# Hybrid streaming encoder on one core: the mixer's key-decay products move from GpSimd to VectorE, ScalarE's exponentials and gates are held in order, norm weights are folded, caches and rotary key go ahead of the query latent

## The chip, the core and the metric

The kernel is one program on one core of a Trainium2 chip. The metric is the device time of one launch in microseconds (us). A core has a matrix engine (TensorE, PE in the tables, with PEld for its weight loads), VectorE (DVE), ScalarE (ACT), GpSimd (POOL) and SyncE (SP), whose queue issues the transfers. Each engine runs its own list of instructions strictly in order; an instruction that has to wait for another engine holds up everything behind it in its list.

## The reference

Two groups of tokens (512 of a new stream, 64 of a running one) pass two layers of an encoder that share all weights. In each layer stand a feed-forward block, a mixer and a second feed-forward block. The mixer projects the normalised input once and splits it among three head groups:

```python
z = h @ w_in[l]
q_a, kv_a, kpe_raw, hq, hf, hi, hg, cu, cv = jnp.split(z, offsets, axis=-1)
# HGRN2, in chunks of 64: b = cumulative sum of log forget gates
diff  = b[:, :, None] - b[:, None, :]
decay = exp(diff) where causal, else 0
A     = einsum('bthe,btshe,bshe->bhts', qc, decay, kc)
S_new = exp(b_last) * S + einsum('bshe,bshd->bhed', kc * exp(b_last - b), vc)
o_b   = rmsnorm(o, out_g) * silu(hg)
# chunk MLP: u = gelu(cu); v = rmsnorm(gelu(cv)) * v_g; o_c = u * (w_s v + b_s)
# latent attention: q from rmsnorm(q_a), keys from rmsnorm(kv_a) and the rotated kpe_raw
mix = concat([o_a, o_b, o_c], axis=-1) @ w_out[l]
```

## The kernel before, in words

All 576 tokens stand as columns; a float32 product is made of three fast products of split operands (`split`: ScalarE writes the high part `hi`, VectorE the rest `lo`; `three`, `nat3`: hi·hi, hi·lo, lo·hi). `together`, `unit` and `natural` multiply by pieces of a weight; `cols`, `nat_chunks` and `chunk` load such a piece (`wr`) and split it into `wh` and `wl`.

The order of the program is made in two steps. The Python code is one main thread that issues matrix products, and a list of generators (`spawn`, `tick`): a generator goes on when the clock `self.t`, an estimate of TensorE's time, has passed the value that it yielded. Then a scheduler of the framework takes all instructions and sets each engine's list by priorities and its own estimates. An instruction passed through `keep_in_program_order` may not move ahead of what the Python code gave the same engine before it.

`mixer` runs in four stages. **First**, `natural` multiplies five tiles of tokens by 512, 512 and 320 columns of `w_in` (tile `n` of TensorE): `vg` (values and gate), `uv` (the chunk MLP's inputs) and the latents of the keys. Beside it runs the generator `hgrn`: the decay matrix A is built by seven levels of halving (`LEVELS`), two halves of the heads each, so 14 items. `make(n)` subtracts the cumulative sum around each block's middle (`e`, two VectorE instructions L701 and L702), takes the exponential on ScalarE (L703), multiplies the keys by it on GpSimd (`w`, L705) and the queries by it on VectorE (`zb`, two instructions L711). `use(n)` multiplies both on TensorE (`lv`, `ls`) and copies the entries of this level into A (L726, L733). `self.pace` is the time between items. **Second**, three `unit` calls make the query latent (`u`); beside them run the states (`su`, `st`), the outputs `out` (`o`, `on`), and `cmlp` (`cm`, `oc`): both call `group_norm`, whose inverse root is made on GpSimd (`rsqrt`, tile `gr`); `to_mix` transposes the results (`tp`). `gates` makes GELU (L882) and SiLU (L886). `latent` makes the key latents (`cn`, `rk`). **Third**, `caches` and `rotary_key` are spawned behind the query latent (`ck`, `kp`, `kd`), then values (`v`) and rotated queries (`rope`: `sw` on ScalarE and GpSimd, `qr`). **Fourth** come `query`, keys, attention and the output projection.

Of the kernel before, what the change touches and what calls it, by code (L numbers as in the profile page):

```python
# [8 lines left out]
F32 = mybir.dt.float32  # L9
# [6 lines left out]
P = 128  # L16
# [33 lines left out]
class Net:  # L50
    def __init__(self, tc, i, o):
        self.tc = tc
        self.nc = tc.nc
        self.i = i
        self.o = o
        self.count = 0
        self.bg = []
        self.t = 0.0
        self.pace, self.apace, self.l1, self.l2, self.l3 = 3.0, 2.16, 1.26, 3.94, 2.15
# [565 lines left out]
    def group_norm(self, src):  # L625
        nc = self.nc
        sq = self.slot("gsq")
        nc.scalar.activation(sq[:, :256], src, AF.Square)
        ss = self.small("gs", 4)
        nc.vector.tensor_reduce(ss, sq[:, :256].rearrange("p (g d) -> p g d", g=4), AX.X, ALU.add)  # L630
        nc.vector.tensor_scalar(ss, ss, 1.0 / 64, EPS, op0=ALU.mult, op1=ALU.add)
        r = self.small("gr", 4)
        self.rsqrt(r, ss, 4)
        return r.unsqueeze(2).to_broadcast([P, 4, 64])

    def to_mix(self, src, k0, i):
        ps = self.sm("tp")
        for e in range(2):
            self.flip(ps[:, e * P:(e + 1) * P], src[:, e * P:(e + 1) * P])
        c, w = tcol(i), twid(i)  # L640
        for e in range(2):
            self.split(self.mixh[k0 + e][:, c:c + w], self.mixl[k0 + e][:, c:c + w], ps[:, e * P:e * P + w])
# [7 lines left out]
    def hgrn(self, l, zq, zf, vg):  # L650
# [36 lines left out]
        for m in range(2):  # L687
            qk.append(self.slot("qk"))
            nc.gpsimd.tensor_tensor(qk[m], q[m], kk[m], op=ALU.mult)
# [3 lines left out]
        def make(n):  # L693
            li, h, m = items[n]
            c0 = 64 if h == 64 else 0
            nb = (T - c0) // (2 * h)
            e = self.slot("e")
            bv = b[m][:, c0:].rearrange("p (b x) -> p b x", x=2 * h)
            ev = e[:, c0:].rearrange("p (b x) -> p b x", x=2 * h)
            rb = bv[:, :, h - 1:h].to_broadcast([P, nb, h])  # L700
            nc.vector.tensor_tensor(ev[:, :, :h], rb, bv[:, :, :h], op=ALU.subtract)  # L701
            nc.vector.tensor_tensor(ev[:, :, h:], bv[:, :, h:], rb, op=ALU.subtract)  # L702
            nc.scalar.activation(e[:, c0:], e[:, c0:], AF.Exp)  # L703
            w = self.slot("w")
            nc.gpsimd.tensor_tensor(w[:, c0:], kk[m][:, c0:], e[:, c0:], op=ALU.mult)  # L705
            z = zbuf[n % 3]
            qv = q[m][:, c0:].rearrange("p (b x) -> p b x", x=2 * h)
            for g in range(2):
                rs = slice(g * 64, (g + 1) * 64)
                zo = z[rs, g, c0 // 2:].rearrange("p (b x) -> p b x", x=h)  # L710
                nc.vector.tensor_tensor(zo, qv[rs, :, h:], ev[rs, :, h:], op=ALU.mult)  # L711
            ready[n] = (w, z)
# [60 lines left out]
        for m in range(2):  # L773
# [5 lines left out]
            nc.scalar.activation(e, e, AF.Exp)  # L779
            eb[m] = self.slot("eb")  # L780
            nc.scalar.activation(eb[m], b[m], AF.Exp)
            nc.gpsimd.tensor_tensor(e, e, kk[m], op=ALU.mult)
# [18 lines left out]
        for i in (1, 2, 3, 4, 0):  # L801
            for m in range(2):
# [16 lines left out]
                yield 0.1  # L819
# [4 lines left out]
        def out(i):  # L824
# [10 lines left out]
            if rows < P:  # L835
# [3 lines left out]
            nc.vector.tensor_tensor(on[:, :256].rearrange("p (g d) -> p g d", g=4),  # L839
                                    ps[:, :256].rearrange("p (g d) -> p g d", g=4), r, op=ALU.mult)  # L840
            nc.vector.tensor_tensor(on[:, :256], on[:, :256], vg[i][:, 256:512], op=ALU.mult)
            yield 7.71
            self.to_mix(on, 4, i)
# [7 lines left out]
    def cmlp(self, l, i, t, c):  # L851
# [3 lines left out]
        vv = v.rearrange("p (g d) -> p g d", g=4)  # L855
        nc.vector.tensor_tensor(vv, vv, r, op=ALU.mult)
        nc.gpsimd.tensor_tensor(v, v, c["vg"], op=ALU.mult)
# [19 lines left out]
    def gates(self, l, c, vg, uv):  # L877
# [3 lines left out]
        for i in range(5):  # L881
            nc.scalar.activation(uv[i][:, :512], uv[i][:, :512], AF.Gelu_apprx_tanh)  # L882
            self.spawn(self.cmlp(l, i, uv[i], c), 0.8 + 2.59 * i)
        for i in range(5):
            g = vg[i][:, 256:512]
            nc.scalar.activation(g, g, AF.Silu)  # L886
            nc.gpsimd.tensor_tensor(g, g, c["og"], op=ALU.mult)
# [3 lines left out]
    def latent(self, l, i, ps, c, r, kr, cth, ctl):  # L891
# [15 lines left out]
        yield 4.0  # L907
# [138 lines left out]
    def mixer(self, l, gpost, gpre, nxt, packed):  # L1046
# [15 lines left out]
        c["og"] = self.gain_rows("hgrn_out_g", l)  # L1062
# [29 lines left out]
        for i in range(5):  # L1092
            ps = self.natural(nch, i, 320)
            lat.append(self.spawn(self.latent(l, i, ps, c, r, kr, cth, ctl)))
            self.step(self.bg[-1])

# [15 lines left out]
        cg = self.spawn(self.caches(l, c), 0.0)  # L1112
        lat.append(self.spawn(self.rotary_key(l, kr, a), 1.0))
# [171 lines left out]
    def bounds(self, more):  # L1285
        nc = self.nc
        ps = self.sm("tp")
        self.flip(ps[:, :18], more)
        nc.vector.tensor_copy(self.colg[:, 96:], ps[:, :18])
# [19 lines left out]
    def build(self):  # L1309
# [10 lines left out]
        pin = tc.keep_in_program_order  # L1320
# [26 lines left out]
        self.colg = const.tile([P, 114], F32, name="colg", tag="colg")  # L1347
# [30 lines left out]
        more = const.tile([18, P], F32, name="more", tag="more")  # L1378
        nc.sync.dma_start(more[0:6], i["mla_qa_g"].rearrange("l (k p) -> (l k) p", p=P))
        nc.sync.dma_start(more[6:10], i["hgrn_lb_logits"].rearrange("l (k p) -> (l k) p", p=P))  # L1380
        nc.sync.dma_start(more[10:18], i["cmlp_b_s"].rearrange("l g t -> (l g) t"))
        self.bs = self.colg[:, 106:114]
        self.spawn(self.pre_stats(0, 0.17, sums))
# [78 lines left out]
```

## Time and profile before

| | us |
|---|---|
| three runs, median (lowest to highest) | 2287.99 (2287.04 to 2290.99) |
| the profiled execution, its own time | 2284.6 |
| its span | 2282.8 |
| TensorE busy in the span | 2214.3 (97%) |
| VectorE busy | 1554.9 (68%) |
| ScalarE busy | 1093.4 (48%) |
| GpSimd busy | 225.6 (10%) |

Between the span and the execution's own time lie 1.8 us of start and end. The two mixers take about 307 us each, from 451 to 757 and from 1575 to about 1890; the other time is feed-forward blocks, where TensorE hardly ever waits. A matrix product's row shows its whole way through the engine, so consecutive rows overlap: what one costs is read from the distance of starts, or from a chain row ("x65" in so many us). "idle before" in square brackets is the time in which the engine had nothing to do, with what ended it. PEclk is the granted clock as a share of full speed.

### The profile page before, as it was taken

To read this page: it belongs to the slowest core of one execution; us is meant where nothing else is said; L and a number is where in the kernel's file an instruction comes from. 1 tells how busy PE (TensorE), PEld (TensorE's weight loads), DVE (VectorE), ACT (ScalarE), POOL (GpSimd) and SP (SyncE) were. 2 spreads that over 40 slices of the span, in tenths; PEclk is the share of its full clock that TensorE was granted. 3 is DMA by queue.
4 is the path that set the end of the run, shared out by engine and by line. 5 is a ranking of instruction groups with operands and counts; after the bars stand their busy time and mean duration, and the time that the engine had idled before them with its cause. 6 is when DMAs were issued, how large, how long until landed. Compare 5 with 4: busy or idle time off the path is not lost.

```text
span 2282.8 us, 39582 instructions
## 1 busy us (share of the span) xinstructions
PE 2214.3 (97%) x15988; PEld 2157.1 (94%) x15988; DVE 1554.9 (68%) x2627; ACT 1093.4 (48%) x1917; POOL 225.6 (10%) x230
## 2 busy tenths in 40 slices
PE   9999999998899999999999999999988999999998
PEld 8999999888799999999999999998887999999998
DVE  6787643787666888845597875447975678887443
ACT  7444442466554644443354444324645645444423
POOL 0000000343301100000020000004332020000000
PEclk9999999999999999999999999999999999999999
DMA  7333442312112333344133334423121232333421
GB/s 218 93 93 93 120 135 84 98 53 78 54 57 79 107 93 93 94 129 125 56 98 93 93 89 133 127 65 102 40 87 48 63 112 72 98 93 101 122 70 42
DMA packets 339531, 211.06 MB, mean 92 GB/s; under 512 B 17378, under 2 KB 319700, under 8 KB 339348
## 3 DMA queue, kind: packets, MB, share of 16 engines
q1 hardware_dynamic: 339348, 208.54, 30.6%
q8 instruction: 125, 2.05, 0.4%
q14 instruction: 58, 0.48, 0.1%
HBM read 190.11 MB, written 18.38 MB: 91 GB/s over the span
## 4 chain that ended last, share of the span: by engine, by line
PE 80%; DVE 10%; ACT 3%; issue 3%; POOL 3%; DMA 0%; SPq 0%; POOLq 0%; DVEq 0%; ACTq 0%
PE d L68 24%; PE X L68 20%; PE Q L68 10%; PE u L68 8%; PE R L68 5%; PE wo L68 4%; DVE zb L711 2%; PE n L68 2%; PE sc L68 1%; DVE x L256 1%; DVE hl L142 1%; DVE d L253 1%; DVE wl L127 1%; PE q L68 1%; PE oT L68 1%
## 5 line engine op out<-in xcount | busy, mean ns | idle before, releaser
L68 PE MATMUL d<-gh,wh 128*128 128x288 f32 x1408 | 413.5, 297 | 2.7 <-ACT gh L138 2.7
L68 PE MATMUL d<-gl,wh 128*128 128x288 f32 x1408 | 413.9, 295 | 0.0
L68 PE MATMUL d<-gh,wl 128*128 128x288 f32 x1408 | 412.7, 294 | 0.0
L127 DVE TENSOR_TENSOR wl<-wr,wh 128x1024 fp32r<-128x1024 f32 (+3 forms) x190 | 224.0, 1183 | 177.7 <-ACT wh L126 176.2
L126 ACT ACTIVATE wh<-wr 128x1024 fp32r<-128x1024 f32 (+3 forms) x190 | 191.5, 1011 | 297.2 <-PE d L68 166.9
L68 PEld LDWEIGHTS d<-gh,wh 128*128 128x128 f32 x1408 | 262.3, 187 | 3.6 <-ACT gh L138 3.6
L68 PEld LDWEIGHTS d<-gh,wl 128*128 128x128 f32 x1408 | 264.8, 188 | 0.0
L68 PEld LDWEIGHTS d<-gl,wh 128*128 128x128 f32 x1408 | 264.1, 188 | 0.0
L68 PE MATMUL X<-th,wh 128*128 128x288 f32 x864 | 255.7, 296 | 0.0
L68 PE MATMUL X<-tl,wh 128*128 128x288 f32 x864 | 254.9, 295 | 0.0
L68 PE MATMUL X<-th,wl 128*128 128x288 f32 x864 | 254.0, 294 | 0.0
L68 PE MATMUL u<-hh,wh 128*128 128x288 f32 x736 | 223.4, 305 | 3.1 <-ACT x L1368 1.5
L138 ACT ACTIVATE wh<-wr 128x1024 fp32r<-128x1024 f32 x144 | 152.1, 1056 | 154.2 <-PE R L68 68.5
L68 PE MATMUL u<-hl,wh 128*128 128x288 f32 x736 | 223.0, 303 | 1.2 <-DVE hl L142 1.2
L68 PE MATMUL u<-hh,wl 128*128 128x288 f32 x736 | 221.7, 302 | 0.0
L139 DVE TENSOR_TENSOR wl<-ws,wh 128x1024 fp32r<-128x1024 f32 x108 | 132.5, 1226 | 100.5 <-ACT wh L138 100.2
L139 DVE TENSOR_TENSOR wl<-wr,wh 128x1024 fp32r<-128x1024 f32 x144 | 175.6, 1222 | 15.8 <-ACT wh L138 14.4
L151 POOL TENSOR_TENSOR p<-m,mhalf 128x3 f32<-128x3 f32 (+1 forms) x14 | 14.4, 1030 | 1713.8 <-DVE m L234 1507.8
L395 DVE TENSOR_TENSOR d<-d,d 128x288 f32<-128x288 f32 x128 | 55.3, 455 | 182.0 <-PE d L68 181.9
L138 ACT ACTIVATE wh<-ws 128x1024 fp32r<-128x1024 f32 x108 | 114.6, 1061 | 132.6 <-DVE ws L502 96.1
L68 PEld LDWEIGHTS X<-th,wl 128*128 128x128 f32 x864 | 162.8, 188 | 0.0
L68 PEld LDWEIGHTS X<-tl,wh 128*128 128x128 f32 x864 | 162.2, 188 | 0.0
(364 smaller groups left out, 5781.8 us busy)
## 6 DMA issues: line engine op xcount, KB each, us to landing
wr<-ffn_w_gate SPq DMA_DIRECT2D x144, 256.0 KB, 3.0
wr<-ffn_w_up SPq DMA_DIRECT2D x144, 256.0 KB, 3.4
wr<-ffn_w_down SPq DMA_DIRECT2D x64, 512.0 KB, 4.2
wr<-w_in SPq DMA_DIRECT2D x30, 512.0 KB, 3.7
xd<-x SPq DMA_DIRECT2D x48, 288.0 KB, 2.4
x<-xd SPq DMA_DIRECT2D x48, 288.0 KB, 5.5
wr<-ffn_w_down SPq DMA_DIRECT2D x32, 384.0 KB, 3.5
wr<-ffn_w_gate SPq DMA_DIRECT2D x16, 512.0 KB, 3.9
```

Of the source, the lines that this page charges most:

```text
L68: self.nc.tensor.matmul(out, lhsT, rhs, start=start, stop=stop, skip_group_check=onto)
L126: nc.scalar.activation(hi[:, :a * b], raw[:, :a * b], AF.Copy)
L127: nc.vector.tensor_tensor(lo[:, :a * b], raw[:, :a * b], hi[:, :a * b].bitcast(F32), op=ALU.subtract)
L138: nc.scalar.activation(hi, src, AF.Copy)
L139: nc.vector.tensor_tensor(lo, src, hi.bitcast(F32), op=ALU.subtract)
L142: nc.vector.scalar_tensor_tensor(lo, src, scale, hi.bitcast(F32), op0=ALU.mult, op1=ALU.subtract)
L151: self.nc.gpsimd.tensor_tensor(out, m, self.mhalf[:, :n], op=ALU.pow)
L253: nc.vector.scalar_tensor_tensor(d[s][:, sl], d[s][:, sl], gpost[s], bc, op0=ALU.mult, op1=ALU.mult)
L256: nc.vector.tensor_tensor(self.x[k][:, sl], self.x[k][:, sl], d[k][:, sl], op=ALU.add)
L395: nc.vector.tensor_tensor(d[m][:, sl], d[m][:, sl], ps[hf][:, :n], op=ALU.add)
L711: nc.vector.tensor_tensor(zo, qv[rs, :, h:], ev[rs, :, h:], op=ALU.mult)
```

## The change

The products of the keys with the decay (L689, L705, L782) go from GpSimd to VectorE; the one of the levels is written over `e` and only into the half of each block that is used, so tile `w` is gone. Five kinds of ScalarE instruction, the exponentials of the levels and of the states, GELU and SiLU, are passed through `keep_in_program_order` (`self.pin`). The norm of each group is applied by four instructions of 64 columns that take the factor and the weight (or the gate) at once. `hgrn_out_g` is no longer multiplied into the gate by GpSimd, but applied as a column scale in `to_mix`'s split. `caches` and `rotary_key` are spawned ahead of the query latent. Four waiting times change: `pace` 3.0 to 2.2, and the yields of the states (0.1 to 0.6), of the latents (4.0 to 8.0) and the rotary key (1.0 to 6.0).

```diff
-        self.pace, self.apace, self.l1, self.l2, self.l3 = 3.0, 2.16, 1.26, 3.94, 2.15
+        self.pace, self.apace, self.l1, self.l2, self.l3 = 2.2, 2.16, 1.26, 3.94, 2.15
...
-    def to_mix(self, src, k0, i):
+    def to_mix(self, src, k0, i, scale=(None, None)):
...
-            self.split(self.mixh[k0 + e][:, c:c + w], self.mixl[k0 + e][:, c:c + w], ps[:, e * P:e * P + w])
+            self.split(self.mixh[k0 + e][:, c:c + w], self.mixl[k0 + e][:, c:c + w], ps[:, e * P:e * P + w], scale=scale[e])
...
-            nc.gpsimd.tensor_tensor(qk[m], q[m], kk[m], op=ALU.mult)
+            nc.vector.tensor_tensor(qk[m], q[m], kk[m], op=ALU.mult)
...
-            nc.scalar.activation(e[:, c0:], e[:, c0:], AF.Exp)
-            w = self.slot("w")
-            nc.gpsimd.tensor_tensor(w[:, c0:], kk[m][:, c0:], e[:, c0:], op=ALU.mult)
+            self.pin(nc.scalar.activation(e[:, c0:], e[:, c0:], AF.Exp))
...
-            ready[n] = (w, z)
+            kv = kk[m][:, c0:].rearrange("p (b x) -> p b x", x=2 * h)
+            nc.vector.tensor_tensor(ev[:, :, :h], ev[:, :, :h], kv[:, :, :h], op=ALU.mult)
+            ready[n] = (e, z)
...
-            nc.scalar.activation(e, e, AF.Exp)
+            self.pin(nc.scalar.activation(e, e, AF.Exp))
...
-            nc.scalar.activation(eb[m], b[m], AF.Exp)
-            nc.gpsimd.tensor_tensor(e, e, kk[m], op=ALU.mult)
+            self.pin(nc.scalar.activation(eb[m], b[m], AF.Exp))
+            nc.vector.tensor_tensor(e, e, kk[m], op=ALU.mult)
...
-            nc.vector.tensor_tensor(on[:, :256].rearrange("p (g d) -> p g d", g=4),
-                                    ps[:, :256].rearrange("p (g d) -> p g d", g=4), r, op=ALU.mult)
-            nc.vector.tensor_tensor(on[:, :256], on[:, :256], vg[i][:, 256:512], op=ALU.mult)
+            for g in range(4):
+                gs = slice(g * 64, (g + 1) * 64)
+                nc.vector.scalar_tensor_tensor(on[:, gs], ps[:, gs], r[:, g:g + 1], vg[i][:, 256 + g * 64:320 + g * 64],
+                                               op0=ALU.mult, op1=ALU.mult)
...
-        nc.vector.tensor_tensor(vv, vv, r, op=ALU.mult)
-        nc.gpsimd.tensor_tensor(v, v, c["vg"], op=ALU.mult)
+        for g in range(4):
+            gs = slice(g * 64, (g + 1) * 64)
+            nc.vector.scalar_tensor_tensor(v[:, gs], v[:, gs], r[:, g:g + 1], c["vg"][:, gs], op0=ALU.mult, op1=ALU.mult)
...
-            nc.scalar.activation(uv[i][:, :512], uv[i][:, :512], AF.Gelu_apprx_tanh)
+            self.pin(nc.scalar.activation(uv[i][:, :512], uv[i][:, :512], AF.Gelu_apprx_tanh))
...
-            nc.scalar.activation(g, g, AF.Silu)
-            nc.gpsimd.tensor_tensor(g, g, c["og"], op=ALU.mult)
+            self.pin(nc.scalar.activation(g, g, AF.Silu))
...
-        yield 4.0
+        yield 8.0
...
+        lat.append(self.spawn(self.rotary_key(l, kr, a), 6.0))
+        cg = self.spawn(self.caches(l, c), 0.0)
...
-        cg = self.spawn(self.caches(l, c), 0.0)
-        lat.append(self.spawn(self.rotary_key(l, kr, a), 1.0))
```

How the lists of the engines change is shown at three places. **VectorE, in the levels of the first mixer**, before: `e` is the difference that goes to the exponential, `zb` the queries times it, `lv` the product of TensorE that is copied into A; `w` is not in this list, since GpSimd makes it.

```order
L711 TENSOR_TENSOR zb_5007<-z_4608,e_5189 64x288 x2
L701 TENSOR_TENSOR e_5222<-b_5025 128x18x16
L702 TENSOR_TENSOR e_5222<-b_5025 128x18x16
L127 TENSOR_TENSOR wl_5561<-wr_5558,wh_5560 128x960
L711 TENSOR_TENSOR zb_5009<-z_4607,e_5222 64x288 x2
```

And of the change:

```order
L726 COPY_PREDICATED at_5119<-lmask_c,lv_5172 128x4x64
L709 TENSOR_TENSOR zb_5010<-z_4608,e_5150 64x288 x2
L711 TENSOR_TENSOR e_5150<-e_5150,k_5012 128x9x32
L726 COPY_PREDICATED at_5121<-lmask_c,lv_5172 128x4x64
L709 TENSOR_TENSOR zb_5006<-z_4609,e_5179 64x288 x2
L711 TENSOR_TENSOR e_5179<-e_5179,k_5016 128x9x32
```

The product with the keys (now L711) stands behind the two of the queries, and each item has one VectorE instruction of 288 columns more.

**ScalarE, from the levels to the gates of the first mixer**, before: `vg` is the gate, `e` the exponential of an item, and each change between their functions is a table load.

```order
L886 ACT_TABLE_LOAD
L886 ACTIVATE vg_5170<-vg_5170 128x256
L703 ACT_TABLE_LOAD
L703 ACTIVATE e_5189<-e_5189 128x576
L126 ACTIVATE wh_5560<-wr_5558 128x960
L126 ACTIVATE wh_5566<-wr_5564 128x640
L703 ACTIVATE e_5222<-e_5222 128x576
L1071 ACTIVATE vg_5230<-n_5172,rn_4456 128x512
L886 ACT_TABLE_LOAD
L886 ACTIVATE vg_5230<-vg_5230 128x256
L703 ACT_TABLE_LOAD
```

And of the change, behind the last level (`kdn`, `kd` are copies of the transposed decayed keys, `gsq` the squares of the first group norm):

```order
L793 ACTIVATE kdn_5707<-tp_5708 128x512
L797 ACTIVATE kd_809_5714<-tp_5715 64x128
L883 ACT_TABLE_LOAD
L883 ACTIVATE uv_5313<-uv_5313 128x512
...
L883 ACTIVATE uv_5567<-uv_5567 128x512
L887 ACT_TABLE_LOAD
L887 ACTIVATE vg_4993<-vg_4993 128x256
...
L887 ACTIVATE vg_5224<-vg_5224 128x256
L628 ACTIVATE gsq_5740<-uv_5313 128x256
```

GELU and SiLU stand in one block of ten instructions with two table loads, behind the last exponential and the first `kdn`, and the first squares of a norm stand behind the block. The whole program has 43 table loads before and 17 now.

**TensorE, at the transposes of the rotary key and the caches of the first mixer**, before: `ss` is the sum for the query norm, `v` the values; all 144 products `u` of the query latent are done.

```order
L73 MATMUL tp_6374<-ident_c,on_6257 128x128 x2
L68 MATMUL ss_6479<-ones,accq_5848 128x1 x6
L73 MATMUL tp_6573<-ident_c,ck_6437 128x128
L73 MATMUL tp_6504<-ident_c,kd_6445 128x128 x3
L68 MATMUL v_6538<-wh_6399,cth_5660 128x512
```

And of the change:

```order
L73 MATMUL tp_6197<-ident_c,oc_6025 128x128 x2
L73 MATMUL tp_6232<-ident_c,kd_6129 128x128 x3
L73 MATMUL tp_6206<-ident_c,ck_6003 128x128 x4
L73 MATMUL tp_6254<-ident_c,kd_6130 128x128 x2
L68 MATMUL u_6306<-hh_4503,wh_6302 128x288
L68 MATMUL u_6306<-hl_4504,wh_6302 128x288
L73 MATMUL tp_6243<-ident_c,kp_6005 128x128 x2
```

These transposes now stand ahead of the second of the three units of the query latent: 48 products `u` are in front of them in the list and 96 behind.

## Rows read from the trace of the kernel before

**Rows 1.** Stages: span; busy PE, PEld, DVE, ACT, POOL; PEclk, DMA, GB/s.
```profile
451.00:553.80 102.80, 97.31 (x532) 84.38 (x531) 83.39 (x148) 65.81 (x96) 36.54 (x29) 0.97 0.21 59
553.80:596.20 42.40, 37.75 (x288) 34.52 (x286) 31.54 (x102) 15.17 (x41) 18.77 (x18) 1.00 0.27 80
596.20:629.10 32.90, 27.68 (x147) 23.96 (x145) 17.75 (x49) 23.65 (x59) 8.26 (x7) 0.84 0.22 65
...
1575.40:1680.30 104.90, 98.63 (x533) 85.72 (x532) 86.10 (x152) 65.77 (x96) 34.97 (x29) 0.95 0.20 58
```

**Rows 2.** Chain that ended last: start us, us, what.
```profile
452.18 14.78 PE n L68 x65
...
793.78 3.20 PE Q L68 x24
```

**Rows 3.** Timeline of TensorE: start, us, what, count, [idle before].
```profile
479.59 1.13 PE L68 MATMUL lv<-zb,w 128*128 128x128 f32 x8 [1.03 <-DVE zb L711]
484.01 1.05 PE L68 MATMUL lv<-zb,w 128*128 128x128 f32 x8
...
488.87 1.13 PE L68 MATMUL lv<-zb,w 128*128 128x128 f32 x8
...
538.48 0.69 PE L73 MATMUL tp<-ident_c,cn 128*128 128x128 f32 x2 [4.46 <-DVE cn L902]
...
1605.26 1.67 PE L68 MATMUL lv<-zb,w 128*128 128x128 f32 x8 [2.32 <-DVE zb L711]
...
1665.04 0.69 PE L73 MATMUL tp<-ident_c,cn 128*128 128x128 f32 x2 [3.95 <-DVE cn L902]
```

**Rows 4.** Busy time behind those waits, columns as in rows 1.
```profile
538.50:544.80 6.30, 6.30 (x28) 6.11 (x28) 2.53 (x9) 1.10 (x5) 0.55 (x1) 0.55 0.27 94
1605.30:1611.40 6.10, 6.10 (x25) 5.22 (x26) 6.05 (x10) 4.37 (x6) 1.96 (x2) 0.72 0.31 86
```

**Rows 5.** Groups by form: busy us, mean ns, idle before; then timeline rows.
```profile
L711 DVE TENSOR_TENSOR zb<-z,e 64x288 f32<-64x288 f32 x48 | 46.8, 975 | 9.4 <-ACT e L703 9.0
L523 DVE TENSOR_TENSOR s<-s,X 128x288 f32<-128x288 f32 x72 | 32.5, 452 | 7.1 <-PE X L68 7.1
L726 DVE COPY_PREDICATED at<-lmask_c,lv 128x256 f32<-128x256 int32 x56 | 25.8, 525 | 5.5 <-PE lv L68 5.4
...
490.56 2.16 DVE L711 TENSOR_TENSOR zb<-z,e 64x288 f32<-64x288 f32 x2
490.38 1.56 POOL L705 TENSOR_TENSOR w<-k,e 128x576 f32<-128x576 f32 x1 [2.44 <-ACT e L703]
```

**Rows 6.** ScalarE: timeline of one change of tables; GELU and SiLU by form.
```profile
481.50 1.00 ACT L126 ACTIVATE wh<-wr 128x960 fp32r<-128x960 f32 x1
482.52 1.28 ACT L886 ACT_TABLE_LOAD   x1
483.81 0.42 ACT L886 ACTIVATE vg<-vg 128x256 f32<-128x256 f32 x1
...
L882 ACT ACTIVATE uv<-uv 128x512 f32<-128x512 f32 x10 | 6.3, 633 | 0.1
L886 ACT ACTIVATE vg<-vg 128x256 f32<-128x256 f32 x10 | 4.2, 418 | 0.2
```

**Rows 7.** Group norms: the root by form, and a timeline row of four.
```profile
L151 POOL TENSOR_TENSOR gr<-gs,mhalf 128x4 f32<-128x4 f32 x20 | 23.6, 1178 | 34.3 <-DVE gs L631 32.1 <-PE u L68 2.0
...
570.18 0.86 DVE L870 SCALAR_TENSOR_TENSOR oc<-cm,colg,uv 128x64 f32<-128x64 f32 x4 [0.21 <-PE cm L68]
```

**Rows 8.** TensorE's waits in the third stage, timeline.
```profile
606.89 0.87 PE L73 MATMUL tp<-ident_c,kd 128*128 128x128 f32 x3 [1.51 <-DVE kd L932]
...
619.29 0.79 PE L68 MATMUL v<-wh,cch 128*128 128x512 f32 x1 [2.02 <-ACT cch L138]
```

**Rows 9.** The rotated queries, by form.
```profile
L1141 ACT ACTIVATE sw<-q 32x288 f32<-32x288 f32 x32 | 12.8, 401 | 0.5
L1150 ACT ACTIVATE qr<-q 64x576 fp32r<-64x576 f32 x8 | 5.5, 684 | 4.2 <-DVE q L1144 4.1
```

More of the change, by code (lines that the diff above doesn't have):

```diff
@@ L633, in group_norm @@
         self.rsqrt(r, ss, 4)
-        return r.unsqueeze(2).to_broadcast([P, 4, 64])
-    def to_mix(self, src, k0, i):
+        return r
+    def to_mix(self, src, k0, i, scale=(None, None)):
         ps = self.sm("tp")
@@ L818, in hgrn @@
                         nc.sync.dma_start(dst, new[s, s])
-                yield 0.1
+                yield 0.6
         while not self.gated:
@@ L838, in out @@
             on = self.slot("on")
-            nc.vector.tensor_tensor(on[:, :256].rearrange("p (g d) -> p g d", g=4),
-                                    ps[:, :256].rearrange("p (g d) -> p g d", g=4), r, op=ALU.mult)
-            nc.vector.tensor_tensor(on[:, :256], on[:, :256], vg[i][:, 256:512], op=ALU.mult)
+            for g in range(4):
+                gs = slice(g * 64, (g + 1) * 64)
+                nc.vector.scalar_tensor_tensor(on[:, gs], ps[:, gs], r[:, g:g + 1], vg[i][:, 256 + g * 64:320 + g * 64],
+                                               op0=ALU.mult, op1=ALU.mult)
             yield 7.71
-            self.to_mix(on, 4, i)
+            self.to_mix(on, 4, i, [self.og[:, 2 * l + e:2 * l + e + 1] for e in range(2)])
             self.left -= 1
@@ L854, in cmlp @@
         r = self.group_norm(v)
-        vv = v.rearrange("p (g d) -> p g d", g=4)
-        nc.vector.tensor_tensor(vv, vv, r, op=ALU.mult)
-        nc.gpsimd.tensor_tensor(v, v, c["vg"], op=ALU.mult)
+        for g in range(4):
+            gs = slice(g * 64, (g + 1) * 64)
+            nc.vector.scalar_tensor_tensor(v[:, gs], v[:, gs], r[:, g:g + 1], c["vg"][:, gs], op0=ALU.mult, op1=ALU.mult)
         if i == 0:
@@ L1060, in mixer @@
         self.left, self.attn_left, self.gated, self.decayed = 10, 20, False, False
-        c["og"] = self.gain_rows("hgrn_out_g", l)
         nch = self.nat_chunks(w, 1216, 512)
@@ L1287, in bounds @@
         ps = self.sm("tp")
-        self.flip(ps[:, :18], more)
-        nc.vector.tensor_copy(self.colg[:, 96:], ps[:, :18])
+        self.flip(ps[:, :22], more)
+        nc.vector.tensor_copy(self.colg[:, 96:], ps[:, :22])
         L = self.colg[:, 102:106]
@@ L1318, in load @@
             return t
-        pin = tc.keep_in_program_order
+        pin = self.pin = tc.keep_in_program_order
         self.ident = load("ident", [P, P])
@@ L1346, in build @@
             self.mul(self.warm[:, :P], self.ones, self.ones, True, True)
-        self.colg = const.tile([P, 114], F32, name="colg", tag="colg")
+        self.colg = const.tile([P, 118], F32, name="colg", tag="colg")
         ps = self.sm("tp")
@@ L1377, in build @@
         self.ahead += [self.cols(*q) for q in todo[2:]]
-        more = const.tile([18, P], F32, name="more", tag="more")
+        more = const.tile([22, P], F32, name="more", tag="more")
         nc.sync.dma_start(more[0:6], i["mla_qa_g"].rearrange("l (k p) -> (l k) p", p=P))
@@ L1381, in build @@
         nc.sync.dma_start(more[10:18], i["cmlp_b_s"].rearrange("l g t -> (l g) t"))
+        nc.sync.dma_start(more[18:22], i["hgrn_out_g"].rearrange("l (k p) -> (l k) p", p=P))
         self.bs = self.colg[:, 106:114]
+        self.og = self.colg[:, 114:118]
         self.spawn(self.pre_stats(0, 0.17, sums))
```

## The prediction, made before the changed kernel ran

> **What bounds the kernel now.** I read the busy times first, then the stretches of a mixer one by one, then the chain and TensorE's timeline, and last the groups by form. TensorE is busy 97% of the span, so only three things can move the time: what TensorE waits for, what its clock loses behind a wait, and its own work, whose instruction counts the change leaves as they are. The feed-forward blocks have hardly a wait and are not touched. The reader is to see in [rows 1] that each mixer has three stretches with a gap between the span and TensorE's busy time: 5.5 us in the first stage of the first mixer and 6.3 of the second, 4.7 in the second stage, 5.2 in the third, where PEclk is 0.84 besides. What TensorE's work itself costs comes from chain rows [rows 2]: a product of 512 columns 14.78/65 = 0.227 us, one of 288 columns 3.20/24 = 0.133.
>
> In the first stage the waits are few and named [rows 3]: 1.03 us for `zb` at the first level of the first mixer and 2.32 in the second, and 4.46 and 3.95 for the normalised latents `cn`, each time released by VectorE. Behind them the granted clock is low [rows 4]: 0.55 over 6.3 us, which costs 6.3 x 0.45 = 2.8, and 0.72 over 6.1, which costs 1.7. This is TensorE partly at its lower level of 1.2 GHz after it had stood idle. For the second mixer's wait for `cn` I take the same 2.8. Between two levels lie 15 products of 512 columns, and the levels start 488.87 - 484.01 = 4.86 us apart.
>
> **First stage, part by part.** The change takes 12 instead of 15 products between the levels, so an item has 4.86 - 3 x 0.227 = 4.18 us of TensorE over it. VectorE has one more product per item (14 in a mixer, 288 columns). Its price depends on one thing: the queries' products `zb` take 0.975 us in the mean, while a product of the same size from another place takes 0.452 [rows 5]. In the timeline such a pair takes 2.16 us just where GpSimd's `w` of 1.56 runs beside it [rows 5]. I read that as the two holding each other up. GpSimd's product is gone, so I take 0.45 for `zb` and the new product alike. One item then costs VectorE 5 x 0.45 (two differences, two `zb`, the new one) + 2 copies x 0.525 [rows 5] + 0.2 for a `ls` copy = 3.5 us, hidden under 4.18. If the cover failed (0.975 stays for `zb` and for the new product) it would be 5.1, 0.9 late per item, 13 times: 12 us per mixer. In the other direction VectorE gives back 28 x 0.52 = 14.6 us per mixer against 6.3 of new products, and that is why I expect the `cn` waits to go: the latents also come later in TensorE's list, with the last 42 products between them and the transposes ahead. What is late next is the first level: its exponential now stands in order behind the state's exponentials and a table load, so I put 1.3 back (a load is 1.28 [rows 6]). Ten transposes of the decayed keys come into this stage and six of the latents leave it, net 0.3. First mixer: -(1.03 + 4.46 + 2.8) + 0.3 + 1.3 = -6.7. Second: -(2.32 + 1.7 + 3.95 + 2.8) + 0.3 + 1.3 = -9.2. Bounds: nothing gained (the wait for `cn` stays, as VectorE carries more) up to -8.3 and -10.8.
>
> Thirteen table loads per mixer leave ScalarE, 13 x 1.28 = 16.6 us. I cost that at nothing: ScalarE is busy 65.8 of 102.8 us there [rows 1], and no wait of TensorE in [rows 3] ends on it. The norm weight in the split's scale and four rows more in a constant table cost nothing visible either: 20 splits keep their number and size.
>
> **Second stage.** Here the order counts. The nine transposes of the rotary key and the caches stood behind all 144 products `u`; now 48 are in front of them and 96 behind. TensorE's list is strict, so these 96 can't start until VectorE has made `kd`, and `kd` stands on VectorE's list behind most of the group norms and states. When VectorE can begin: the gates are one block now. Behind the first transposed decayed keys come the copy of 0.59, two loads 2.57 [rows 6], five GELU 5 x 0.633 and five SiLU 5 x 0.418 [rows 6], and only then the first squares: 8.4 us, which end about 0.3 us before the last products of the first stage. What VectorE has to do until `kd`: 12 sets of four instructions of 64 columns at 0.86 [rows 7], 10.3; 20 state updates at 0.86/4, 4.3; four weight remainders of some 640 columns, by columns from the 0.452 for 288, 4.0; some 53 small instructions at 0.2, an estimate from the same 0.86/4, 10.6. Sum 29.2. VectorE can't run without gaps, since each norm goes to GpSimd and back. Its busy share was 31.54/42.4 = 0.74 in this stage and 83.39/102.8 = 0.81 in the first [rows 1], the one in which TensorE waited for it; I take 0.81, and keep 0.74 and 0.90 for the range: 36 us (39.5 and 32.4). TensorE then has, behind `kd`, the nine transposes 1.2, 96 x 0.133 = 12.8, seven pairs of late transposes 1.7, and 1.0 for the clock (between 0 and the 2.8 above, low because the waits come in pieces). Stage: -0.3 + 36 + 1.2 + 12.8 + 1.7 + 1.0 = 52.4, against 42.4 before: +10.0 in each mixer (+13.5 at 0.74, +6.4 at 0.90). That is the price of the new order, and the largest term.
>
> At one place the Trainium skill would have it otherwise. The trace shows a table load that starts 0.02 us after the end of the activation ahead (482.50) and is followed by the next activation 1.29 after its start [rows 6]. "ScalarE: Activation LUTs", section "What ACT_TABLE_LOAD costs", adds a drain of about 1.38 us to the 1.283 of the load, 2.66 for each change of tables. The load agrees and the drain isn't in the row. By the rule the two loads ahead of the first norm would take 5.3 and not 2.57, each mixer would be 2.75 later, and the sum 5.5 us higher, about 2284.6.
>
> **Third stage.** The waits for `kd` (1.51) and for the caches' split `cch` (2.02) [rows 8] go, since both are made a stage earlier: -3.5 at least. At most TensorE's work at full clock is left, 27.68 x 0.84 = 23.3 of 32.9: -9.6. Not all of it comes, because the rotated queries hang on ScalarE: 16 x 0.401 + 4 x 0.684 = 9.2 us per mixer [rows 9], with GpSimd and VectorE between. I take the middle, -6.5 in each.
>
> **Sum.** First mixer -6.7 + 10.0 - 6.5 = -3.2; second -9.2 + 10.0 - 6.5 = -5.7; together -8.9. The profiled execution took 2284.6 (span 2282.8 and 1.8 around it): 2275.7. The median of the runs is 2287.99, 3.4 above that execution, so I forecast 2275.7 + 3.4 = 2279.1.
>
> **The rivals.** (B) *TensorE stays the bound in the second stage.* For it: TensorE was busy 37.75 of 42.4 there, with VectorE beside it at 31.54, and VectorE begins with less behind it, as its stretched products are gone. Then the stage grows by only about 1 us for moved transposes: -6.7 + 1.0 - 6.5 = -12.2 and -9.2 + 1.0 - 6.5 = -14.7, in all -26.9: 2261. Against it: two thirds of the query latent can't start before `kd`.
> (C) *The group norms hold VectorE, and the kernel is slower.* The root on GpSimd takes 1.178 us in the mean and stands between two instructions of VectorE [rows 7]; GpSimd stood idle 34.3 us ahead of these roots, 32.1 of it for VectorE, so the two wait for each other in turn. With the norms behind the block of gates, eight of them come one after another; each 0.8 us longer than I count makes 6.4, and a clock loss of 2.6 more (the 2.8 of [rows 4] instead of part of it) makes 45 instead of 36: +19 per mixer, in all +9.1, so 2297. It decides from the point at which `kd` is ready: the sum is zero at 40.5 us behind the end of the first stage's products, and beyond 42.8 the kernel is slower by more than can be told from nothing. Against it: the chain's pieces overlap in the stage before, with a share of 0.74.
> (D) *The change does not do what it says.* The stretched `zb` were not GpSimd's doing; then VectorE has 5.1 us per item against 4.18, 12 us per mixer as above: 2303. Against it: the 2.16 and the 1.56 start within 0.2 us of each other [rows 5].
>
> **How the numbers follow.** About 0.2%, 4.6 us, is what a measurement of this kernel can tell from no change; the band is 2283.4 to 2292.6. Forecast 0.48, own range 2271 to 2288 (shares 0.90 to 0.74 give 2272 to 2286); of it 0.31 is faster and 0.17 the same. B 0.24, all faster. C 0.20, of which 0.03 the same and 0.17 slower. D 0.08, slower. Faster 0.55, same 0.20, slower 0.25. The range is 2259 to 2302: B with half of its lower side, the forecast, C but for its tail.
>
> **What would show it.** Step one: `zb` at about 0.45 us in the groups by form, no idle time in front of the first `cn` transposes, levels 4.2 us apart. If `zb` stays near 0.97, D holds. Step two: a wait of TensorE for `kd` or for group norms in the stretch behind the first stage, which is then 50 to 55 us long with VectorE above 0.8; without that wait, B holds; with over 56 us and waits on GpSimd's root, C. Step three: no wait for `kd` and `cch` behind the query latent, and 26 us where there were 33. The forecast is wrong if the second stage doesn't grow by 6 to 14 us, or if new waits stand in the fourth stage, which I cost at nothing because its order on TensorE is the same.

## The result and the profile after

| | before | after |
|---|---|---|
| median (lowest to highest), us | 2287.98 (2287.04 to 2290.99) | 2301.26 (2299.79 to 2301.62) |
| ratio, 95% interval | | 1.0059 (1.0047 to 1.0071) |
| span of the profiled execution | 2282.8 | 2299.8 |

The changed kernel is 13.3 us slower; the forecast was 8.9 faster. The stages of the two mixers say where. They are cut on TensorE's timeline at the first product `n` behind the transposes `bc` (some 1 us after the very first `n`), the end of the last `n`, the first `v` and the first `sc`:

| us | before | after | difference | forecast |
|---|---|---|---|---|
| first stage | 101.8, 103.9 | 96.5, 96.0 | -5.3, -7.9 | -6.7, -9.2 |
| second stage | 42.5, 42.7 | 61.7, 60.0 | +19.3, +17.3 | +10.0, +10.0 |
| third stage | 36.2, 37.8 | 31.0, 32.0 | -5.2, -5.8 | -6.5, -6.5 |

Two of the three stages went as forecast. The second grew by nearly twice as much. These stages add 12.4 us; the other 4.6 of the 17.0 between the two spans lie outside them (below). The spans are 17.0 us apart and the medians 13.3, as the profiled execution of the kernel before was 3.4 us below its median.

The busy times by stage, columns as in [rows 1] (span; busy PE, PEld, DVE, ACT, POOL; PEclk; DMA share; GB/s), after. The first row begins at the very first `n`:

```profile
453.80:551.30 97.50, 96.01 (x540) 82.61 (x539) 72.40 (x160) 47.77 (x79) 3.88 (x6) 1.00 0.21 60
551.30:613.00 61.70, 49.69 (x299) 44.20 (x298) 41.67 (x164) 19.99 (x66) 12.82 (x15) 0.75 0.23 66
613.00:644.00 31.00, 27.38 (x153) 24.28 (x152) 12.57 (x24) 21.16 (x44) 6.46 (x5) 0.89 0.16 54
...
1687.20:1747.20 60.00, 48.81 (x299) 43.66 (x298) 41.59 (x164) 20.03 (x65) 12.80 (x15) 0.77 0.22 63
```

In the first stage hardly 1.5 us are left between the span and TensorE's busy time, and PEclk is 1.00. In the second, TensorE has 299 products where [rows 1] has 288 in nearly the same part, yet it is busy 11.9 us longer (49.69 against 37.75), because PEclk is 0.75 and not 1.00. Idle time grew from 4.7 to 12.0. So of the +19.3 about 7 are idle time of TensorE and 12 are longer busy time at a lower clock. That says where TensorE spent the time, not yet what set the end: up to `kd` it waits for VectorE again and again, and faster products there could have ended in longer waits.

The clock piece by piece, same columns:

```profile
565.00:570.00 5.00, 3.60 (x31) 3.41 (x29) 3.94 (x16) 2.58 (x7) 1.01 (x1) 1.00 0.07 21
570.00:575.00 5.00, 3.32 (x14) 2.50 (x13) 4.05 (x18) 0.22 (x1) 1.53 (x2) 0.60 0.43 124
575.00:580.00 5.00, 4.25 (x18) 3.83 (x18) 3.30 (x12) 0.51 (x3) 0.00 (x0) 0.50 0.73 209
...
590.50:596.00 5.50, 2.68 (x10) 1.65 (x11) 3.32 (x17) 1.04 (x3) 2.01 (x2) 0.50 0.13 27
596.00:602.00 6.00, 6.00 (x27) 5.97 (x28) 3.42 (x14) 1.48 (x7) 1.01 (x1) 0.52 0.00 0
602.00:613.00 11.00, 11.00 (x86) 10.92 (x86) 6.32 (x16) 7.08 (x21) 1.84 (x2) 1.00 0.15 49
```

The granted clock falls to 0.50, TensorE's level of 1.2 GHz, at about 571 us, just behind idle pieces of 1.40 and 0.89 (below), and stays there until after 601. In the last piece at that level TensorE is busy without a gap and still makes 27 products in 6 us, afterwards 86 in 11; most of both are `u`, which start 0.24 us apart there and 0.13 afterwards.

What it waited for, TensorE's timeline (start, us, what, count, [idle before <- releaser]):

```profile
568.86 1.07 PE L68 MATMUL cm<-uv,wt 128*128 128x64 f32 x8 [1.40 <-DVE st L815]
571.10 0.79 PE L68 MATMUL su<-vg,kd 64*128 64x128 f32 x2 [0.89 <-DVE oc L871]
575.15 0.80 PE L68 MATMUL o<-st,qe 128*128 128x128 f32 x2 [0.94 <-DVE cn L902]
581.84 1.97 PE L68 MATMUL cm<-uv,wt 128*128 128x64 f32 x8 [1.46 <-DVE ctl L139]
588.77 0.69 PE L73 MATMUL tp<-ident_c,oc 128*128 128x128 f32 x2 [1.66 <-DVE ml L139]
590.48 0.88 PE L73 MATMUL tp<-ident_c,kd 128*128 128x128 f32 x3 [1.02 <-DVE kd L932]
595.84 0.58 PE L68 MATMUL u<-hh,wh 128*128 128x288 f32 x1 [1.99 <-DVE on L841]
...
637.15 0.58 PE L68 MATMUL k<-cch,wh 128*128 128x256 f32 x1 [2.78 <-ACT v L1165]
```

There is no long wait for `kd`, as I had imagined it; there are eleven between 0.2 and 2.0 us, 11.9 in all, each released by VectorE, whatever TensorE's next instruction was. The wait for `kd` that [rows 8] shows in the third stage has moved here (1.02). At the end of the third stage there is now one of 2.78 for ScalarE, in both mixers; before, the same place had 0.95 in the second mixer and none in the first.

ScalarE and VectorE where the norms begin, timelines with the same columns:

```profile
542.03 1.28 ACT L883 ACT_TABLE_LOAD   x1
543.32 2.72 ACT L883 ACTIVATE uv<-uv 128x512 f32<-128x512 f32 x5
546.04 1.28 ACT L887 ACT_TABLE_LOAD   x1
547.34 1.65 ACT L887 ACTIVATE vg<-vg 128x256 f32<-128x256 f32 x5
548.89 0.40 ACT L628 ACTIVATE gsq<-uv 128x256 f32<-128x256 f32 x1
```

```profile
549.32 0.42 DVE L630 TENSOR_REDUCE gs<-gsq 128x4 f32<-128x256 f32 x1 [7.14 <-ACT gsq L628]
549.78 0.17 DVE L631 TENSOR_SCALAR gs<-gs 128x4 f32<-128x4 f32 x1
551.08 0.87 DVE L858 SCALAR_TENSOR_TENSOR uv<-uv,gr,cmlp_v_g 128x64 f32<-128x64 f32 x4 [1.13 <-POOL gr L151]
```

VectorE stands idle for 7.14 us until the block of ten gates is through; TensorE is still covered by products `n` then, but VectorE begins the norms only as these run out.

Forms that answer to [rows 5] and [rows 7] (busy us, mean ns | idle before):

```profile
L709 DVE TENSOR_TENSOR zb<-z,e 64x288 f32<-64x288 f32 x48 | 21.7, 451 | 1.0 <-ACT e L703 0.5
L711 DVE TENSOR_TENSOR e<-e,k 128x288 f32<-128x288 f32 x24 | 11.1, 460 | 0.3
L841 DVE SCALAR_TENSOR_TENSOR on<-o,gr,vg 128x64 f32<-128x64 f32 x40 | 8.7, 278 | 7.6 <-POOL gr L151 6.7 <-DMA out_hgrn_s<-st 0.9
L151 POOL TENSOR_TENSOR gr<-gs,mhalf 128x4 f32<-128x4 f32 x20 | 20.2, 1010 | 72.7 <-DVE gs L631 67.6 <-DVE kss L897 2.7 <-PE tp L73 2.4
```

`zb` takes 0.451 us where it took 0.975, and the new product 0.460. The root on GpSimd is not longer than before, 1.010 against 1.178. The transposes of the first `cn` start with no idle time ahead, both here and in run e7 below (its row second):

```profile
549.82 0.44 PE L73 MATMUL tp<-ident_c,cn 128*128 128x128 f32 x2
```

```profile
537.56 0.38 PE L73 MATMUL tp<-ident_c,cn 128*128 128x128 f32 x2
```

VectorE between 549.7 us and `kd` at 590.5 (columns as in [rows 1]), and four of its waits of the second stage, all ahead of `kd` (waiting <- releaser: us in total, times, longest):

```profile
549.70:590.50 40.80, 31.52 (x190) 27.15 (x189) 29.04 (x121) 11.99 (x40) 8.98 (x11) 0.76 0.30 83
```

```profile
DVE uv L858 <- POOL gr L151: 4.0, 5, 1.1
...
DVE st L815 <- PE su L68: 2.1, 2, 1.6
DVE ctl L139 <- ACT cth L138: 2.1, 2, 1.9
DVE oc L871 <- PE cm L68: 1.3, 1, 1.3
```

### The profile page after: what moved, and what is told of

Its sections match the earlier page's. It is cut to its first block, busy times and chain, and to the rows that moved or that the text cites. A ratio compares the mean times of both kernels' runs of the same rounds, so it can differ in the third digit from the quotient of the medians.

```text
span 2299.8 us, 39529 instructions
## 1 busy us (share of the span) xinstructions
PE 2226.5 (97%) x15988; PEld 2165.0 (94%) x15988; DVE 1535.9 (67%) x2713; ACT 1060.9 (46%) x1891; POOL 145.8 (6%) x174
## 4 chain that ended last, share of the span: by engine, by line
PE 85%; DVE 7%; ACT 3%; POOL 2%; issue 2%; DMA 1%; SPq 0%; POOLq 0%; DVEq 0%; ACTq 0%
PE d L68 24%; PE X L68 20%; PE Q L68 10%; PE u L68 9%; PE R L68 5%; PE n L68 5%; PE wo L68 4%; PE sc L68 1%; DVE x L256 1%; DVE hl L142 1%; PE lv L68 1%; DVE d L253 1%; PE q L68 1%; PE oT L68 1%; POOL acc L198 1%
## 5 line engine op out<-in xcount | busy, mean ns | idle before, releaser
L68 PEld LDWEIGHTS X<-th,wh 128*128 128x128 f32 x864 | 161.9, 187 | 0.0
```

Source lines behind the costliest of these rows:

```text
L68: self.nc.tensor.matmul(out, lhsT, rhs, start=start, stop=stop, skip_group_check=onto)
```

## The experiments

Two theories of the second stage were set against each other first. O: the order, with `u` behind the transposes of `kd` and `ck`. G: the block of gates, which holds up the norms. Kernels were run in groups of four on one chip beside the kernel before; since the chips differ a little, the ratios to the kernel before are compared, and 0.001 is 2.3 us. Times laid beside an expectation are the ratio times 2288. Stages come from one profiled execution of each kernel.

**e1, caches and rotary key behind the query latent again.**

```diff
-        lat.append(self.spawn(self.rotary_key(l, kr, a), 6.0))
-        cg = self.spawn(self.caches(l, c), 0.0)
...
+        cg = self.spawn(self.caches(l, c), 0.0)
+        lat.append(self.spawn(self.rotary_key(l, kr, a), 1.0))
```

> The changed kernel with one part undone: caches and rotary key are spawned behind the query latent again, with the rotary key's old wait. Theory O (the 96 products u that stand behind the transposes of kd and ck are the loss): the second stage falls from 61.8 and 60.1 us back to about 43, the third grows by 5.3 and 5.8, so 2301 - 18.8 - 17.1 + 11 = 2276. Theory G (the loss is made ahead of kd, since the block of ten gates holds up all group norms and TensorE has only the first 48 u beside it): only what lies behind 588.5 us can come back, some 5 us per mixer, and the third stage takes as much again, so 2296 to 2302.

Ratio 1.0029 (1.0015 to 1.0043): 7 us of the changed kernel's loss come back, less than O and a little more than G wanted. Second stages 52.9 and 53.3, third 34.0 and 34.3.

**e2, the gates not held in order.**

```diff
-            self.pin(nc.scalar.activation(uv[i][:, :512], uv[i][:, :512], AF.Gelu_apprx_tanh))
+            nc.scalar.activation(uv[i][:, :512], uv[i][:, :512], AF.Gelu_apprx_tanh)
...
-            self.pin(nc.scalar.activation(g, g, AF.Silu))
+            nc.scalar.activation(g, g, AF.Silu)
```

> The changed kernel with one part undone: GELU and SiLU are no longer held in program order on ScalarE; the exponentials still are, and 41 table loads stand in the program instead of 17. Theory G: the first squares of a group norm no longer stand behind the block of ten gates, VectorE's idle 7.1 us ahead of the first one goes and the cm and su products spread into the end of the first stage; the second stage is 8 to 12 us shorter in each mixer, so about 2281. Theory O: the wait for kd stays, VectorE is as late with it, at most 3 us per mixer: 2295 to 2301.

Ratio 1.0021 (1.0009 to 1.0034), 9 us back, again between the two. The second stage is 50.9 and 49.8, but the first 100.8 and 99.9: four of the eleven microseconds only moved, as products `su` and `cm` now stand among the `n`.

**e3, both undone.**

> Both parts undone at once. Theory G: as with the gates free alone, a few us less or more, 2276 to 2283. Theory O: as with the late caches alone, 2276. If the two only cost when together (a block that delays kd, and u that wait for kd), both single undoings give the whole of it and this one is no better than either; if they add, it is faster than both, towards 2268.

Ratio 0.9959 (0.9946 to 0.9971). This is 23 us below the changed kernel, more than the two single steps together (16), though the difference of 7 is good to 6 only. Neither theory alone is right: order and block each cost, and undone together they give at least their sum. The second stage of the first mixer, and of e1 for comparison (columns as above):

```profile
552.00:604.90 52.90, 45.73 (x288) 41.23 (x286) 37.32 (x147) 18.22 (x59) 12.83 (x15) 0.81 0.23 61
```

```profile
555.40:596.60 41.20, 36.14 (x270) 34.37 (x269) 29.02 (x108) 15.45 (x49) 9.45 (x10) 0.96 0.25 74
```

Between them only the ten gates are free. Idle time is 7.2 in the first (e1) and 5.1 in the second (e3); the rest of the difference is clock, 0.81 against 0.96, and 18 products fewer. Those stand in the first stage now, which is 4.4 and 4.1 us longer in e3 than in e1, so of the 11.7 and 11.9 us that the second stage loses 7 to 8 are won.

**e4, the order alone, on the kernel before.** The two lines that e1 takes out are put in.

> The kernel before with one part of the change alone: caches and rotary key spawned ahead of the query latent, with the change's wait of 6.0. Theory O: the wait for kd comes with this part, the second stage grows by 15 or more and the third shrinks by 5, so 2305 to 2310. Theory G: the norms begin as early as before, the transposes find kd ready or nearly so; the third stage shrinks by about 5 in each mixer and the second grows by the 1.2 of the moved transposes, so 2280 to 2288.

Ratio 1.0048 (1.0030 to 1.0066), 11 us slower: the order costs by itself, without block or norms. Its second stage, and the piece of it that is slow:

```profile
554.50:607.10 52.60, 47.20 (x301) 43.73 (x301) 36.63 (x124) 17.23 (x53) 19.68 (x18) 0.84 0.24 75
...
585.00:596.00 11.00, 11.00 (x55) 11.00 (x53) 6.43 (x23) 2.10 (x8) 4.21 (x4) 0.50 0.20 63
```

```profile
569.02 0.49 PE L73 MATMUL tp<-ident_c,kd 128*128 128x128 f32 x3
```

`kd` was ready 14.5 us into the stage, with no wait for it (last row). TensorE's idle time is 5.4 us against 4.7 before; the other 9 us are the lower clock. It lasts from about 582 to 600, where TensorE is busy 17.56 of 18.00 us, first with `o`, `cm` and the transposes of `oc` alone, products of 64 and 128 columns, because the `u` that stood among them had been given out earlier. As TensorE hardly waits there, the clock lengthens this stage directly, other than in the changed kernel ahead of `kd`.

**e5 and e6, more products for TensorE.** The changed kernel and e4 with four products ahead of each `o` and `cm`:

```diff
             ps = self.mm("o")
+            for _ in range(4):
+                nc.tensor.matmul(ps[:, :288], self.hpart(0, 0)[0][:, :P], self.hpart(0, 1)[0], start=True, stop=True)
```

> The changed kernel with four products of 288 columns more ahead of each o and each cm in the second stage (80 in the program, 10.6 us at full clock; what they write is overwritten by o and cm). Theory C (most of the loss is TensorE's clock: 0.50 from about 572 to 599 us, while only small products and waits stand there): the clock stays at 1.00 for longer, 10 us or more of the low stretch come back in each mixer, the products fill part of the idle time, so 2285 to 2296. Theory W (the waits for VectorE set the end, the clock follows them and costs nothing of its own): not faster than the changed kernel, 2301 to 2311.

> The kernel of run e4 (the kernel before with caches and rotary key ahead of the query latent) with the same 80 products. There TensorE idled hardly more than before the part was made (5.4 us in the second stage against 4.7), yet the stage was 10 us longer, with a granted clock of 0.50 from 585 to 596. Theory C: the clock stays up, 9 us come back and 5.3 go to the products in each mixer: 2286 to 2291. Theory W: 2300 to 2307, as the products only add.

Ratios 1.0068 (1.0051 to 1.0086) and 1.0045 (1.0028 to 1.0061): no faster than without them. e5 is as theory W has it; e6, 2298, lies between the two, nearer to W, and is no slower than e4 either, though 10.6 us of products were put in. Yet the clock of the first mixer's second stage rose, from 0.75 to 0.83 in e5 and from 0.84 to 0.91 in e6 (columns as above):

```profile
550.80:612.50 61.70, 51.76 (x339) 46.95 (x338) 41.68 (x164) 20.05 (x66) 12.83 (x15) 0.83 0.24 66
```

```profile
553.60:608.70 55.10, 49.61 (x341) 45.92 (x340) 36.40 (x124) 17.27 (x53) 19.73 (x18) 0.91 0.23 71
```

In e6 (second fence) clock worth 8.4 - 5.0 = 3.4 us came back and 5.3 us of products went in; it didn't pay. In e5 `kd` comes 40.0 us behind the last `n`, with a clock of 0.87 up to there, and in the changed kernel 39.2 behind it, with 0.75: a higher clock did not bring it forward, though the added products take time of their own. The stage stays at 61.7 in the first mixer and grows from 60.0 to 66.0 in the second. What the clock would cost with the waits unchanged can't be told apart with such products.

**e7, the key-decay products alone, on the kernel before; e8, the shorter distance too.**

```diff
-            w = self.slot("w")
-            nc.gpsimd.tensor_tensor(w[:, c0:], kk[m][:, c0:], e[:, c0:], op=ALU.mult)
...
+            kv = kk[m][:, c0:].rearrange("p (b x) -> p b x", x=2 * h)
+            nc.vector.tensor_tensor(ev[:, :, :h], ev[:, :, :h], kv[:, :, :h], op=ALU.mult)
+            ready[n] = (e, z)
```

> The kernel before with one part of the change alone: the key-decay products on VectorE, in place; all waiting times as before. Theory Z (GpSimd's products stretched those of VectorE): zb falls from 0.975 to 0.45 us, the waits for cn (4.46, 3.95) go with the low clock behind them, so 7 us in the first mixer and 9 in the second: 2270 to 2275. Theory V (VectorE only has more to do, the waits for cn grow): 2288 to 2300.

> As e7, and the time between the items 2.2 instead of 3.0. If the first stage's gain needs the shorter distance of the levels, this is faster than e7 by 3 or more; if not, within 2 of it, or slower, since the outputs o then stand together behind the first stage with no products u between them, and the clock falls there (theory C): 2278 to 2286.

Ratios 0.9932 (0.9917 to 0.9946) and 0.9925 (0.9908 to 0.9941): 15.6 and 17 us faster. That is theory Z (2270 to 2275; 2272 came). e7's stages are 95.8, 42.6, 36.2 and 95.4, 42.4, 36.0, so nearly all of it is the first stage, shorter by 6.0 and 8.5; the third is 1.8 shorter in the second mixer. The distance of the levels adds nothing that can be measured. In e8 the last `n` ends 14.7 us later than in e7, the outputs `o` stand among the `n`, and the granted clock stays at 1.00: the fall that was feared for them didn't come. e7's `zb`:

```profile
L709 DVE TENSOR_TENSOR zb<-z,e 64x288 f32<-64x288 f32 x48 | 21.7, 452 | 0.8 <-ACT e L703 0.5
```

The Trainium skill, "SBUF — State Buffer", section "SBUF: two separate sides", says that a VectorE instruction with two operands in SBUF and a GpSimd instruction that reads SBUF exclude each other for a whole instruction. The trace agrees: 0.975 us in the mean beside the GpSimd products, 0.452 without them.

**e9 to e12, one part more on e7.** e9 has the norms in four instructions of 64 columns, e10 both moved parts, e11 the rotary key alone ahead of the query latent, e12 the caches alone:

```diff
+        lat.append(self.spawn(self.rotary_key(l, kr, a), 6.0))
...
-        lat.append(self.spawn(self.rotary_key(l, kr, a), 1.0))
```

> The kernel of run e7 (key-decay products on VectorE, ratio 0.9932 to the kernel before) and one part more: each norm applied by four instructions of 64 columns. VectorE's time per norm: four at 0.86 us against two of 256 columns at 0.42 to 0.43 in the on, and one against four in the uv, whose weight was GpSimd's. If VectorE's list sets the second stage, its 2 us more (5 x 0.4) per mixer come through: 3 to 4 slower than e7; if they are hidden, within 1.5 of e7.

> The kernel of run e7 and caches and rotary key ahead of the query latent. If the cost of this order is its own (three pairs of kernels so far give 10 to 13 us), it is 2284 to 2287; if it came only from VectorE being late with its levels (which the key-decay products mend), within 3 of e7, 2272 to 2278.

> The kernel of run e7 with the rotary key alone ahead of the query latent; the caches stay behind it. Nine instructions of VectorE (2.2 us) and five transposes move. If the cost goes with the VectorE work that is moved: about 4 to 5 slower than e7, 2279. If it is the place at which TensorE has no u left to do (the caches take their buffers and transposes there), 2272 to 2277.

> The kernel of run e7 with the caches alone ahead of the query latent; the rotary key stays behind it. Some 3 us of VectorE's splits and six transposes move. By VectorE's work: 5 to 6 slower than e7, 2280. If the small products o and cm that are left without u among them are the cause (they stand less together here than with both parts moved): 2272 to 2278.

| | ratio (95%) | second stages | third stages |
|---|---|---|---|
| e7 | 0.9932 (0.9917 to 0.9946) | 42.6, 42.4 | 36.2, 36.0 |
| e9 norms | 0.9964 (0.9948 to 0.9980) | 45.5, 45.8 | 36.6, 36.5 |
| e10 both | 0.9983 (0.9971 to 0.9995) | 53.6, 51.5 | 30.3, 31.4 |
| e11 rotary key | 0.9911 (0.9891 to 0.9930) | 46.6, 48.5 | 30.7, 30.7 |
| e12 caches | 0.9949 (0.9931 to 0.9967) | 47.4, 48.8 | 33.6, 33.2 |

The norms came out at 7 us where 3 to 4 were expected, good to 5; the profiled execution of e9 was 4.7 us above its median, so its stages read rather long. Their rows on VectorE explain the smaller number: four instructions of 64 columns take as long as the two of 256 that `on` had, and 0.45 us more than the one that `uv` had, 4.5 us in the program.

e10 is as expected if the order has a price of its own (2284), e12 within its second theory (2276), and e11 below both of its theories (2268). The last three rows answer where the gain of the third stage goes. The second stage's price, rotary key and caches apart and then together, is 4.0, 4.8 and 11.0 in the first mixer, more than the sum, and 6.1, 6.4 and 9.1 in the second, less than the sum but more than either. The third stage's gain does not add up at all: the rotary key alone brings 5.5 and 5.3, the caches alone 2.6 and 2.8, both 5.9 and 4.6. So the rotary key alone costs about what it brings. e11 is the fastest kernel here, 2266.64 us beside 2287.32, 0.9% below the kernel before; that it is faster than e7 itself isn't shown, as the two differ by 0.0021 and each ratio is good to 0.0015 to 0.002. The second and third stage of e11, and those of e10:

```profile
548.20:594.80 46.60, 40.06 (x293) 36.78 (x292) 34.52 (x120) 16.09 (x49) 16.08 (x17) 0.96 0.27 74
594.80:625.50 30.70, 27.29 (x166) 24.68 (x166) 16.26 (x38) 24.87 (x58) 8.00 (x7) 0.94 0.22 67
```

```profile
547.70:601.20 53.50, 46.94 (x300) 43.43 (x299) 36.12 (x124) 17.31 (x53) 16.91 (x17) 0.84 0.25 72
601.20:631.50 30.30, 26.60 (x158) 23.86 (x157) 14.72 (x34) 23.60 (x54) 8.13 (x7) 0.94 0.16 55
```

Idle time in the second stage is 6.5 and 6.6 us, alike. The clock isn't: 0.96 against 0.84 (rows of e11 first). In the second mixer it is 0.93 against 0.83, with idle times of 7.5 and 4.7.

## Why the prediction was wrong

**First stage: right.** The step "zb at 0.45" and the waits for `cn` that go with GpSimd's products came out in the changed kernel (0.451; no idle time ahead of the first `cn`; levels 4.1 us apart) and alone in e7. Rival D falls. The size was -13.2 for -15.9 in the changed kernel, -14.5 in e7, which keeps the old distance of the levels.

**Third stage: right.** By the cut that the prediction used, from the first `v` to the `q` behind the keys of the caches (`k<-cch`), it is 26.0 and 26.1 us where it was 32.9 in both mixers, so -6.9 for -6.5; by the table's cut at `sc` -5.2 and -5.8. The "middle" between -3.5 and -9.6 was chosen without a row of its own, so that it fits so well is luck in part. ScalarE does hold the end of the stage, as I argued, but by its copy of the values (2.78 us) and not by the rotated queries that I named.

**Second stage: the step that failed.** Its terms one by one, for the first mixer. VectorE's work until `kd` was sized at 29.2 us, and the trace has 29.04 busy from 549.7 to 590.5. VectorE began its norms at 549.3, 2.0 us ahead of the end of the last product `n` and not 0.3. From there I gave it 36 us until `kd`, at "its busy share ... I take 0.81"; it took 41.2, at a share of 0.71, below both rows that I weighed. Its waits in that time are 4.9 us for roots from GpSimd (`gr`, `rk`), 3.4 for TensorE (`su`, `cm`) and 2.3 for ScalarE. So `kd` came 39.2 us behind the last `n` and not 35.7: 3.5 us of the error.

Behind `kd` I put 16.7 us: 15.7 of products and transposes, nothing for waits, and "1.0 for the clock (between 0 and the 2.8 above, low because the waits come in pieces)". It took 22.5: 2.8 us of waits for `on` and another 4.2 by which the lower clock stretched TensorE's busy time (half of 2.68 us, then 0.48 of 6.00), which leaves 15.5 for the work. That is the other 5.8 us, and the larger error. I took a clock loss to be something that follows one long wait, in proportion to it; here the lower level stood for about 30 us, through pieces with waits and through pieces without. In the second mixer `kd` came 40.3 us behind the last `n` and 19.7 were left behind it, so there the busy share was the larger error.

Ahead of `kd` the lower clock stands for 19.5 us more, and I had no term for it. What it cost there isn't shown: VectorE's own waits for TensorE are the 3.4 us above, and ScalarE, for which it waited 2.3, may have waited for TensorE in turn.

**The causes, by the single edits.** Keys on VectorE -15.6 us (e7). Both moved parts +11.0 on the kernel before (e4), +11.7 on e7 (e10), +6.9 and +14.2 in the changed kernel with the gates held and free (after against e1, e2 against e3). Norms of 64 columns +7.3 (e9). Gates in one block +8.7 with the moved parts (after against e2) and +16 without (e1 against e3). Each is good to about 3 to 5 us. The other parts (exponentials held in order, the distance of the levels, the yields of the states and the latents, the norm weight in the split) show no price: e3, which has them all on top of e9, is at 0.9959 where e9 is at 0.9964. The forecast had the first two: -15.9, and +20 - 13 = +7 for the moved parts. It gave the other two no price of their own: the norms stood only in VectorE's sum, and the block's 8.4 us of ScalarE were right in length (first squares at 548.9) but taken to be free, because TensorE still had `n` to do. VectorE hadn't; it lost 7.14 us.

**The rivals.** B falls: the second stage grew by 19.3 and 17.3 us where B had 1.0. C gave 2297 with +19 in the second stage, and the stage passed C's mark of 56 us. Its mechanism is only half right: VectorE did wait for the roots, 4.0 us in five waits for `gr`, but the roots were not longer, and `kd` came 39.2 and 40.3 us behind the last `n`, at or ahead of C's zero point of 40.5 and not at the 45 that its +19 needs. What C lacked is the time behind `kd`; that its total for the stage is so near is luck. So is it that 2301.3 still lies in the stated range of 2259 to 2302, whose upper end is C's.

**The table loads.** The sentence on the drain is settled by the rows of the block: the load starts 0.02 us after the copy ahead of it ends, at 542.03, and the next activation stands 1.29 behind its start. 26 fewer loads (17 against 43) gave no time that can be seen: e3, with 41 loads again, is faster than e1 with 17. The two differ in the place of the gates too, so the loads have no price of their own here.

**What stays open.** Of the span's 17.0 us, 4.6 lie outside the three stages. The fourth stage is not among them: from the first `sc` to the last product of the output projection it takes 99 us in both kernels and both mixers, as forecast. The first `n` begins 2.8 us later, and pieces of 1.5 come and go at the passages between blocks. In the other profiles this start lies between 450.9 and 455.6 and doesn't follow the edits; its cause wasn't tried. The gates held in order on e7 alone were not tried, nor was e11 with the other parts. How much of the second stage the clock by itself costs was not isolated: e5 and e6 raise it only together with more work.

## What to carry to other kernels

Where two engines hold each other up, take one of them away as an edit of its own and measure it before others are bound to it: here 15.6 us of gain were hidden under 29 us of loss. Large products that lie among small dependent ones are worth keeping there: in e4, giving them out early left TensorE with the small ones alone at half its clock. Work that is moved forward takes a price where it arrives, and each piece adds to it (e10 to e12), while the gain where it left may end at the next engine's limit: the rotary key alone brought what both parts brought.

## What the runs showed of the hardware

Two things were not expected. TensorE at its level of 1.2 GHz stayed there through 11 us in which its busy time was without a gap (585 to 596 in e4, 55 products, granted clock 0.50); what stood there were small products of 64 and 128 columns. And four VectorE instructions of 64 columns take 0.87 us, 0.281 for the single one in the mean, where one of 256 takes 0.425 in the kernel before; four times 0.281 is 1.12, so neighbours overlap by some 0.08 us. The norm of `uv`, before and after:

```profile
L856 DVE TENSOR_TENSOR uv<-uv,gr 128x256 f32<-128x256 f32 x10 | 4.3, 425 | 5.9 <-POOL gr L151 5.7
```

```profile
L858 DVE SCALAR_TENSOR_TENSOR uv<-uv,gr,cmlp_v_g 128x64 f32<-128x64 f32 x40 | 8.7, 281 | 8.1 <-POOL gr L151 8.1
```
